# A hybrid attention and RWKV step on one core: half of the top-k rounds of three query tiles move behind attention's scores

## The chip, the cores and the metric

The kernel runs on one core of a Trainium2 chip. That core has five engines that work side by side, each through its own queue in order: TensorE (PE, matrix products and transposes), VectorE (DVE), ScalarE (ACT), GpSimd (POOL), and SyncE (SP), which here issues DMAs. The metric is the device time of one execution in microseconds (us); lower is better.

## The reference, cut to what matters

One layer of a streaming encoder is computed for 1024 prompt frames and 32 sample frames (1056 rows, in nine row tiles: tiles 0 to 7 of 128 prompt rows, tile 8 of the 32 sample rows).

```python
z = rms_norm(x) @ w_in                       # split into q, k, v, indexer q/k/w, RWKV inputs zs
# group A: sparse attention, 8 query heads, 4 key heads
score[t, s] = sum_h w[t, h] * relu(qi[t, h] . ki[s] / 8)     # admissible keys of the chunk only
keep the 256 best keys of each query (136 for the sample rows' 544 keys)
o_att = softmax(q . k / 8 over the kept keys) @ v
# group B: RWKV-7, 8 heads, a 64x64 state per head that goes through the frames in order
S = S * w_t - (S @ kk_t) b_t + v_t k_t ;  y_t = S @ r_t
h = x + concat(o_att, o_rwkv) @ w_out
y = h + square(relu(rms_norm(h) @ w_ff1)) @ w_ff2
```

For 1024 prompt keys the count kept is min(256, 1024/4) = 256; for the sample rows it is min(256, 544/4) = 136.

## The kernel before, in words

**Stages.** (1) Norm, transposes and the projection, all as products of a high and a low part (three matmuls for one); in it the indexer scores of tiles 2 to 8 (`idx_tile`), the q and k rows (`main2`, `norm_tile`) and the 14 blocks of RWKV inputs (`main3`, `zs_block`, L441 with the two evictions L450 and L451 on ACT). (2) Attention and RWKV side by side. (3) The output projection (L1310), then the feed-forward part (L1374, L1394), which is about half of the time and is not touched.

**Top-k by rounds.** The 256th best score of every row is found bit by bit. A round compares all scores of a tile with a candidate, counts, and sets one bit; there are 31 rounds after a first count. Two groups of tiles do it: `SLS[0]` = tiles 2, 3, 4 and 8 count on VectorE (L343, four counts a round), `SLS[1]` = tiles 5, 6 and 7 count on ScalarE as sums of signs (L363, three activations a round, over 768, 896 and 1024 columns). After the counts three small VectorE operations make the next candidate (L365, L366, L368). `step(1)` is called once behind each row tile of `main2` and each block of `main3` and advances both groups by one round. At the end of each group its masks are made: for tiles 5 to 7 a count, a compare and a minimum (L343, L382, L383), then signs and squares on ScalarE (L397, L398) and a prefix sum and a compare on VectorE (L403, L404), and last the mask `mb` itself (L405). `masks()` runs what is left of both groups before the joint loop of stage 2. In it the scores lie in the tile `G` (tiles 4 to 8), and the mask code works in `S.eq`, which lies in the pool from which RWKV's odd units take their tile `KB`; RWKV's odd units take their big tile `G` from the room of the scores.

**Attention** (`attn_all`) goes through 36 items, a head group j (0 to 3) and a row tile each: for each j the tiles in the order `ORD` = 8, 0, 1, 2, 3, 4, 5, 7, 6. At tile 8 and tile 0 of each j, `prep` loads and transposes that group's keys (L1116, L1118, L1121, L1122). An item makes scores (PE L1153, L1154; DVE L1156 with the mask; exp on ACT L1159), turns them (PE L1177; eviction L1178 on ACT or DVE) and multiplies by the values (L1193).

**RWKV** goes through five units (four of 256 frames, one of 32). Each has a front (gates, decays, the tiles `KB`, `AR`, the products L715 evicted by L718), a triangular inverse (`lane_inverse`: transposes L833 on DVE, 30 small steps L840 and L842 on POOL, transposes L845 and L846 on DVE), a finish on PE of tiny matmuls (L856, L862; DVE L857, L866, L871), a join (L771, L779), and a back with a serial chain over four chunks of 64 frames. `rwkv_tokens` turns the keys of a chunk for the back: eight transposes of 64 partitions (L749) in two groups, each with a copy of its own (L750).

**Order.** The code hands out one piece of attention and one piece of RWKV in turn (the loop at the end of `body`); a scheduler in the framework then fixes the order of each engine's queue by priorities and its own timing. Each queue is worked through in that order.

Of the kernel before, what the change touches and what calls it, by code (L numbers as in the profile page):

```python
# [151 lines left out]
def phase_a(S, pwx, pwy, pa, pi, px, xp, ps, late):  # L152
# [77 lines left out]
    S.sc, c = {}, 0  # L230
    for t in range(4, NT):
        n = 664 if t == 8 else 128 * (t + 1)
        S.sc[t] = G[:, c:c + n]
        c += n
# [3 lines left out]
    for SL in SLS:  # L238
        X = K()
        TK.append(X)  # L240
        X.SL, X.exact = SL, SL is SLS[0]
        for a, d in (("cnt", F32), ("nac", I32), ("cnd", I32), ("cns", F32), ("need", F32)):
            setattr(X, a, S.tk.tile([128, len(SL)], d, name=a + str(len(SL))))
        X.off = S.tk.tile([128, 2, len(SL)], F32, name="off" + str(len(SL)))
# [94 lines left out]
    def count(X, op, get, sc):  # L339
        for j, t in enumerate(X.SL):  # L340
            r = rows_of(t)
            n = S.sc[t].shape[1]
            nc.vector.tensor_scalar(junk[:r, :n], sc[t][:r, :n], get(j, r), None, op0=op, op1=ALU.add,  # L343
                                    accum_out=X.cnt[:r, j:j + 1])

    def topk(X):
# [9 lines left out]
        for i in range(30, -1, -1):  # L356
            if X.exact:
                count(X, ALU.is_lt, c_of, S.sc)
            else:
                for j, t in enumerate(X.SL):  # L360
                    r = rows_of(t)
                    n = S.sc[t].shape[1]
                    nc.scalar.activation(junk2[:r, :n], S.sc[t][:r, :n], AF.Sign, bias=c_of(j, r), scale=-1.0,  # L363
                                         accum_out=cnt[:r, j:j + 1])
            nc.vector.tensor_tensor(nac, cnt, X.off[:, 0] if X.exact else X.off[:, 1], op=ALU.is_gt)  # L365
# [26 lines left out]
        for j, t in enumerate(X.SL):  # L392
# [3 lines left out]
            cum = S.eq[j % 2][:r, :g.shape[1]]  # L396
# [61 lines left out]
    def main():  # L458
# [5 lines left out]
        for X in TK:  # L464
            nc.gpsimd.memset(X.cnt, 0.0)
            nc.gpsimd.memset(X.cns, 0.0)
            for j, t in enumerate(X.SL):
                n = S.sc[t].shape[1]
                for i in range(2):
                    nc.gpsimd.memset(X.off[:, i, j:j + 1], float(n - 256 - 256 * i))  # L470
# [83 lines left out]
    def masks():  # L554
        for g in tk:
            for _ in g:
                pass
# [317 lines left out]
def rwkv_back(S, rp, ps, U, state):  # L875
# [23 lines left out]
    for c in range(NC):  # L899
# [23 lines left out]
        for hp in range(4):  # L923
            for par in range(2):
                nc.tensor.matmul(pS[PAR[par], hp], KBs[:, par, hp], VU[:, par, hp], start=True, stop=True)  # L925
# [172 lines left out]
def attn_all(S, ap, ps):  # L1098
# [3 lines left out]
    items = [(j, t) for j in range(4) for t in ORD]  # L1102
# [40 lines left out]
    def scores(k, h):  # L1143
# [6 lines left out]
        for i, c0 in enumerate(range(0, n, 512)):  # L1150
# [5 lines left out]
            nc.vector.tensor_tensor_reduce(out=s[:, c0:c1], in0=pd, in1=S.mb[t][:, c0:c1], op0=ALU.add, op1=ALU.min, scale=-1.0,  # L1156
                                           scalar=m[:, 0:1] if i else FMAX, accum_out=m[:, i:i + 1])
        i = 1 if n > 512 else 0
        nc.scalar.activation(s, s, AF.Exp, bias=m[:, i:i + 1], scale=-1.0, accum_out=w.m[:, 6 + h:7 + h])  # L1159
# [44 lines left out]
    def begin(k):  # L1204
        j, t = items[k]
        if t == 8 or t == 0:
# [236 lines left out]
ORD = [8,0,1,2,3,4,5,7,6]  # L1443
# [21 lines left out]
def body(tc, I, O, dbg=None):  # L1465
# [4 lines left out]
    with pool(name="const") as cp, pool(name="dram", space=DRAM) as dp:  # L1470
# [16 lines left out]
        S.xs = mp.tile([128, 8, 64], F32R, name="mb7")  # L1487
        p1a, S.tk = opened("p1a", "right")
# [54 lines left out]
        for i in range(EARLYF, max(AHEAD, MA)):  # L1543
            if i == MA:
                masks()
            next(gr)
        if MA >= AHEAD:
            masks()
# [43 lines left out]
```

## Time and profile before

| | |
|---|---|
| median of 3 runs | 1783.88 us (1782.97 to 1784.06) |
| profiled execution | 1782.01 us |
| its span, first to last instruction | 1780.2 us |
| mean granted TensorE clock | 0.937 of full speed |
| busy: PE, DVE, ACT, POOL | 1667.3 us (94%), 913.7 us (51%), 711.4 us (40%), 533.1 us (30%) |

The times of runs agree within 0.1%. The profiled execution lies 1.8 us above its span and 1.9 us below the median. TensorE's clock has two levels, 1.2 and 2.4 GHz; a granted clock of 0.50 in a stretch means 1.2 GHz all through, 1.00 means 2.4 GHz. A matmul at 1.2 GHz is counted busy for longer, so that busy time times granted clock is the work at full speed.

### The profile page before, as it was taken

The page shows a single profiled execution, that of the slowest core. Times are in us where ns is not written, and L with a number is a line of the kernel's source. Part 1 is how long each engine was busy: PE and PEld are TensorE (multiplying, and loading weights), DVE is VectorE, ACT ScalarE, POOL GpSimd, SP SyncE. Part 2 cuts the span into 40 slices and gives each one's busy share as a digit, 9 for nine tenths or more (in the row PEclk, how much of TensorE's full clock was granted, in tenths as well). Part 3 has the DMA queues.
Part 4 walks back from the last instruction along what each step waited for, and adds up shares of the span by engine and source line. Part 5 has one row for each costly group of instructions (what it writes and reads, how often), then busy time and mean ns, then how long its engine had stood idle before and what let it go on. Part 6 is the DMA issues. An engine that isn't in the chain of part 4 may idle for free.

```text
span 1780.2 us, 32465 instructions
## 1 busy us (share of the span) xinstructions
PE 1667.3 (94%) x12966; PEld 1514.6 (85%) x12966; DVE 913.7 (51%) x2016; ACT 711.4 (40%) x1559; POOL 533.1 (30%) x759
## 2 busy tenths in 40 slices
PE   7999979987679999989989999999999999999999
PEld 6787769986557877767767799999999999999998
DVE  6476899975878586675643533232322222222224
ACT  6365567797555453434621331212222221212120
POOL 7568863453303031122210031212122222222110
PEclk9999989996669597988989999999999999999999
DMA  7211131323101102021234241111111111111105
GB/s 219 56 36 44 40 91 61 102 70 100 31 25 30 30 21 70 17 96 45 70 85 144 90 128 53 41 54 42 49 47 48 37 54 42 54 42 48 37 17 171
DMA packets 161087, 112.77 MB, mean 63 GB/s; under 512 B 31632, under 2 KB 150120, under 8 KB 160936
## 3 DMA queue, kind: packets, MB, share of 16 engines
q1 hardware_dynamic: 152104, 106.37, 20.5%
q10 hardware_dynamic: 8832, 4.33, 0.9%
q8 instruction: 102, 1.67, 0.4%
q14 instruction: 49, 0.40, 0.1%
HBM read 85.65 MB, written 25.01 MB: 62 GB/s over the span
## 4 chain that ended last, share of the span: by engine, by line
PE 50%; DMA 2%; ACT 1%; DVE 1%; issue 1%; SPq 0%; POOL 0%; ACTq 0%; DVEq 0%; POOLq 0%
PE pd L1374 20%; PE pr L1394 10%; PE pc L1394 5%; PE po L1394 5%; PE pd L1310 3%; PE pr L1310 2%; DMA of<-od 1%; PE po L1193 1%; DMA w1r<-in_w_ff_dram 0%; PE ptr L1177 0%; PE ptr L1408 0%; PE pc L925 0%; PE pd L1153 0%; PE ptr L145 0%; ACT G L1276 0%
## 5 line engine op out<-in xcount | busy, mean ns | idle before, releaser
L1374 PE MATMUL pd<-hh,w1h 128*128 128x352 f32 x768 | 248.0, 323 | 2.6 <-issue 1.5
L1374 PE MATMUL pd<-hh,w1l 128*128 128x352 f32 x768 | 247.6, 322 | 0.6 <-DVE w1l L1241 0.6
L1374 PE MATMUL pd<-hl,w1h 128*128 128x352 f32 x768 | 246.8, 321 | 0.0
L1380 DVE TENSOR_TENSOR h2l<-rl,h2h 128x352 fp32r<-128x352 f32 x96 | 56.8, 592 | 276.7 <-ACT h2h L1379 276.7
L1240 ACT CAST w2h<-w2r 128x512 fp32r<-128x512 f32 x64 | 39.8, 621 | 293.9 <-PE po L1394 144.7
L1378 POOL TENSOR_TENSOR rl<-rl 128x352 f32<-128x352 f32 x96 | 85.3, 889 | 214.8 <-ACT rl L1377 214.8
L1374 PEld LDWEIGHTS pd<-hh,w1h 128*128 128x128 f32 x768 | 144.1, 188 | 3.5 <-issue 1.8
L1374 PEld LDWEIGHTS pd<-hh,w1l 128*128 128x128 f32 x768 | 144.2, 188 | 0.9 <-DVE w1l L1241 0.9
L1374 PEld LDWEIGHTS pd<-hl,w1h 128*128 128x128 f32 x768 | 144.7, 188 | 0.0
L1241 POOL TENSOR_TENSOR w2l<-w2r,w2h 128x512 fp32r<-128x512 f32 x32 | 41.5, 1298 | 299.3 <-ACT w2h L1240 299.3
L1394 PE MATMUL pr<-h2h,w2l 128*128 128x352 f32 x384 | 124.3, 324 | 0.0
L1394 PE MATMUL pr<-h2h,w2h 128*128 128x352 f32 x384 | 124.3, 324 | 0.0
L1394 PE MATMUL pr<-h2l,w2h 128*128 128x352 f32 x384 | 124.1, 323 | 0.0
L363 ACT ACTIVATE AR<-G,cnd 128x768 bf16<-128x768 f32 (+2 forms) x93 | 96.8, 1040 | 42.4 <-DVE cnd L368 33.9
L1377 ACT ACTIVATE rl<-pd 128x352 f32<-128x352 f32 x96 | 44.3, 463 | 141.9 <-PE pd L1374 135.3
L1400 DVE TENSOR_TENSOR ya<-ya,pr 128x352 f32<-128x352 f32 x84 | 43.8, 521 | 100.6 <-PE pr L1394 100.6
L1177 PE MATMUL ptr<-ident,s 128*128 128x128 f32 (+2 forms) x328 | 66.3, 304 | 18.7 <-ACT s L1159 9.5
L1159 ACT ACTIVATE s<-s,m 32x544 f32<-32x544 f32 (+8 forms) x72 | 55.5, 771 | 56.2 <-DVE m L1156 54.5
L1379 ACT CAST h2h<-rl 128x352 fp32r<-128x352 f32 x96 | 46.6, 485 | 75.5 <-POOL rl L1378 75.5
L1394 PEld LDWEIGHTS pr<-h2l,w2h 128*128 128x128 f32 x384 | 72.3, 188 | 0.1
L1394 PEld LDWEIGHTS pr<-h2h,w2h 128*128 128x128 f32 x384 | 72.2, 188 | 0.1
L1394 PEld LDWEIGHTS pr<-h2h,w2l 128*128 128x128 f32 x384 | 72.3, 188 | 0.1
(452 smaller groups left out, 4573.6 us busy)
## 6 DMA issues: line engine op xcount, KB each, us to landing
w1r<-in_w_ff_dram SPq DMA_DIRECT2D x32, 512.0 KB, 4.2
w2r<-in_w_ff_dram SPq DMA_DIRECT2D x64, 256.0 KB, 2.8
zsd<-zm SPq DMA_DIRECT2D x12, 528.0 KB, 2.8
wraw<-in_w_in_dram SPq DMA_DIRECT2D x24, 256.0 KB, 2.7
wraw<-in_w_in_dram SPq DMA_DIRECT2D x40, 128.0 KB, 2.3
x<-in_x_prompt_dram SPq DMA_DIRECT2D x8, 512.0 KB, 4.9
hres<-hd ACTq DMA_DIRECT2D x16, 256.0 KB, 3.1
out_dram<-hres SPq DMA_DIRECT2D x16, 256.0 KB, 2.3
```

What stands on the lines that cost most here:

```text
L363: nc.scalar.activation(junk2[:r, :n], S.sc[t][:r, :n], AF.Sign, bias=c_of(j, r), scale=-1.0, accum_out=cnt[:r, j:j + 1])
L1159: nc.scalar.activation(s, s, AF.Exp, bias=m[:, i:i + 1], scale=-1.0, accum_out=w.m[:, 6 + h:7 + h])
L1177: nc.tensor.transpose(p[:x, i, h, :r], w.s[h][:, c0 + i * 128:c0 + i * 128 + x], S.ident[:r, :r])
L1241: (nc.vector if i % 2 else nc.gpsimd).tensor_tensor(lo, raw, hi.bitcast(F32), op=ALU.subtract)
L1310: nc.tensor.matmul(acc[:r], a[:, k], b, start=(i == 0), stop=(i == 23))
L1374: nc.tensor.matmul(acc, a[:, k], m[:, k, o:o + n], start=(i == 0), stop=(i == 23))
L1377: nc.scalar.activation(rl, acc, AF.Relu)
L1378: nc.gpsimd.tensor_tensor(rl, rl, rl, op=ALU.mult)
L1379: nc.scalar.copy(h2h[:, o:o + n], rl)
L1380: nc.vector.tensor_tensor(h2l[:, o:o + n], rl, h2h[:, o:o + n].bitcast(F32), op=ALU.subtract)
L1394: nc.tensor.matmul(acc, a[:, k], m[:, o:o + n], start=(i == 0), stop=(i == 11))
L1400: nc.vector.tensor_tensor(y, y, acc, op=ALU.add)
```

## The change

Five edits go together.

1. The scores of tiles 5, 6 and 7 get a tile of their own, `late`, that lives as long as the masks; `G` holds only tiles 4 and 8. Room for it comes from a smaller DMA scratch area (`dynamic_dma_scratch_size=1024`).
2. The rounds of tiles 5 to 7 are advanced at every second call of `step` only, 16 steps (a first count and 15 rounds) in place of 32. The other 16 rounds and the masks become a generator `gm` in the joint loop: one piece at every fifth turn, queued on DVE and ACT behind the last scores and the last exp that were handed out (`issue_after`). Its scratch comes from attention's pool (`junk`, and the tiles `s`, which attention's scores also use).
3. Attention's items get another order, `PASSES`: j = 0 and 1 with tiles 8, 0 to 4 only, j = 2 and 3 with all tiles, then j = 0 and 1 with tiles 5, 7, 6. The keys of j = 0 and 1 are loaded and turned a second time for that (two more `prep`).
4. The exact rounds on VectorE keep the count of scores at or above the candidate and need two small operations in place of three.
5. `rwkv_tokens` turns the keys of both parities at once: four transposes of 128 partitions and one copy of 512 columns per chunk, in place of eight of 64 and two copies of 256.

```diff
     G = S.tk.tile([128, 4096], F32, name="G")
-    for t in range(4, NT):
-        n = 664 if t == 8 else 128 * (t + 1)
-        S.sc[t] = G[:, c:c + n]
+    S.sc, c = {4: G[:, 0:640], 8: G[:, 640:1304]}, 0
+    for t in SLS[1]:
+        n = 128 * (t + 1)
+        S.sc[t] = S.late[:, c:c + n]
...
         for i in range(30, -1, -1):
             if X.exact:
-                count(X, ALU.is_lt, c_of, S.sc)
+                count(X, ALU.is_ge, c_of, S.sc)
+                nc.vector.tensor_scalar(nac, cnt, 255.5, float(1 << i), op0=ALU.is_lt, op1=ALU.mult)
+                nc.vector.scalar_tensor_tensor(cnd, nac, (1 << i) >> 1, cnd, op0=ALU.bitwise_xor, op1=ALU.bitwise_xor)
+                yield
+                continue
...
-                    nc.scalar.activation(junk2[:r, :n], S.sc[t][:r, :n], AF.Sign, bias=c_of(j, r), scale=-1.0,
+                    j2 = junk2 if i > LATE else S.at.tile([128, 1024], BF16, name="junk", bufs=1)
+                    nc.scalar.activation(j2[:r, :n], S.sc[t][:r, :n], AF.Sign, bias=c_of(j, r), scale=-1.0,
...
-                e = S.eq[j % 2][:r, :n]
+                e = S.at.tile([128, 1024], F32, name="s", bufs=XPB)[:r, :n]
...
-    left = [32 - EARLY * (len(IDXO) - EI), 32]
+    left, calls = [32 - EARLY * (len(IDXO) - EI), 31 - LATE], [0]
     def step(n):
+        calls[0] += 1
         for i, g in enumerate(tk):
-            m = min(n, left[i])
+            m = min(n if i == 0 else calls[0] % 2, left[i])
...
     def masks():
-        for g in tk:
-            for _ in g:
-                pass
+        for _ in tk[0]:
+            pass
+        return tk[1]
...
-    KBs = rp.tile([128, 2, 4, 64], F32, name="KBs", bufs=TOKB)
+    KBs = rp.tile([128, 4, 2, 64], F32, name="KBs", bufs=TOKB)
-    for par in range(2):
-        p = ps.tile([128, 4, 64], F32, name=TOKP[0], bufs=TOKP[1])
-        for hp in range(4):
-            nc.tensor.transpose(p[:, hp], U.KB[PAR[par], c, hp].rearrange("p a b -> p (a b)"), S.ident[PAR[par], PAR[par]])
-        nc.scalar.copy(KBs[:, par], p)
+    p = ps.tile([128, 4, 2, 64], F32, name=TOKP[0], bufs=TOKP[1])
+    for hp in range(4):
+        nc.tensor.transpose(p[:, hp].rearrange("p a b -> p (a b)"), U.KB[:, c, hp].rearrange("p a b -> p (a b)"), S.ident)
+    nc.scalar.copy(KBs, p)
...
-    items = [(j, t) for j in range(4) for t in ORD]
+    items = [(j, t) for j, s in PASSES for t in s]
...
+        S.pace = v.ins, a.ins
...
+EARLIER, LATER = (8, 0, 1, 2, 3, 4), (5, 7, 6)
+PASSES = ((0, EARLIER), (1, EARLIER), (2, EARLIER + LATER), (3, EARLIER + LATER), (0, LATER), (1, LATER))
+LATE = 15
+PACE = 5
...
-        gens = [ga, gr]
+        gens, turns = [ga, gr, gm], 0
         while gens or wo is None:
+            turns += 1
             for g in list(gens):
+                if g is gm:
+                    if turns % PACE == 0 or ga not in gens:
+                        with tc.issue_after(S.pace[0]), tc.issue_after(S.pace[1]):
+                            if next(g, 1) == 1:
+                                gens.remove(g)
+                    continue
```

Three places show what the order of the queues becomes. The first is ACT's queue where the projection ends. `zm` and `tm` are the last evictions of RWKV inputs, `AR<-G` the sign counts of tiles 5 to 7, `tmp<-k` and `tmp<-pr` the first steps of RWKV's second unit. Before:

```order
L451 ACTIVATE tm<-acc,pv 96x351
L363 ACTIVATE AR,cnt_121<-G,cnd_123 128x768
L363 ACTIVATE AR,cnt_121<-G,cnd_123 128x896
L363 ACTIVATE AR,cnt_121<-G,cnd_123 128x1024
L363 ACTIVATE AR,cnt_121<-G,cnd_123 128x768
L636 ACTIVATE tmp<-k,pv 128x256 x4
L363 ACTIVATE AR,cnt_121<-G,cnd_123 128x896
L632 ACTIVATE tmp<-pr,hv 128x256 x2
```

Now, at the same place:

```order
L458 ACTIVATE tm<-acc,pv 96x351
L644 ACTIVATE tmp<-k,pv 128x256 x4
L640 ACTIVATE tmp<-pr,hv 128x256 x4
L640 ACTIVATE tha<-pr,hv 128x256 x4
L672 ACTIVATE Ep<-D_4707 128x1040
```

The sign counts are gone from there, and RWKV's second unit follows the evictions directly.

The second place is DVE's queue around the end of the finish of RWKV's first unit (`X` is its last transpose). `KB` with `need` or a scan is mask work of tiles 5 to 7 before; the operations on `KB<-k` and `KB<-tha` are the second unit's. Before:

```order
L871 STREAM_TRANSPOSE X_5393<-G 32x512
L400 TENSOR_SCALAR need_125<-need_125 128x1
L1200 TENSOR_TENSOR t_5691<-t_5691,po 128x128
L404 SCALAR_TENSOR_TENSOR KB<-KB,need_125,G 128x1024
L1163 RECIPROCAL m<-m 128x2
L1141 SCALAR_TENSOR_TENSOR Q<-ptr,Q 64x256
L1178 COPY ph<-ptr 128x256
L684 TENSOR_TENSOR KB<-k,D_4838 64x4x4x64
```

Now, between the same finish's first eviction (L864) and its last transpose (L878), `cnt`, `nac` and `cnd` belonging to one late round:

```order
L864 TENSOR_TENSOR L<-pr,lm 128x512
L1164 ISA s,m<-pd,mb_73 128x256
L1164 ISA m 128x1
L1164 ISA s,m<-pd,mb_73 128x256
L1164 ISA m 128x1
L1172 RECIPROCAL m<-m 128x2
L1209 TENSOR_TENSOR t_5451<-t_5451,po 128x128
L372 TENSOR_TENSOR nac_123<-cnt_122,off_127 128x3
L373 SCALAR_TENSOR_TENSOR cnd_124<-nac_123,cnd_124 128x3
L375 TENSOR_SCALAR cnd_124<-cnd_124 128x3
L873 TENSOR_TENSOR G<-pr,Yl 32x16x32 x4
L878 STREAM_TRANSPOSE X_5221<-G 32x512 x2
```

The wide mask operations have left this place; three small ones of a round have come. The second unit's `KB` now stands before the finish.

The third place is ACT's queue during the first pass of attention, where `junk<-late` are the sign counts of two late rounds and `s` the exps of tiles 3 and 4. Now:

```order
L1167 ACTIVATE s,m<-s,m 128x512 x2
L370 ACTIVATE junk,cnt_122<-late,cnd_124 128x768
L927 COPY VU<-pc 64x256
L370 ACTIVATE junk,cnt_122<-late,cnd_124 128x896
L1148 ACTIVATE Q<-ptr 64x256
L1208 COPY t_5674<-po 128x128
L1187 COPY ph<-ptr 128x512
L370 ACTIVATE junk,cnt_122<-late,cnd_124 128x1024
L1167 ACTIVATE s,m<-s,m 128x640
L370 ACTIVATE junk,cnt_122<-late,cnd_124 128x768
L370 ACTIVATE junk,cnt_122<-late,cnd_124 128x896
L370 ACTIVATE junk,cnt_122<-late,cnd_124 128x1024
```

Before, no count stood among the exps of these tiles; now three stand behind the exps of most items of the first two passes.

## Rows read from the trace of the kernel before

**Rows 1.** Windows by stage: us, busy and count of PE, PEld, DVE, ACT, POOL; clock; DMA.

```profile
209.00:414.00 205.00, 183.77 (x1081) 174.66 (x1079) 175.92 (x475) 163.21 (x353) 99.33 (x119) 0.95 0.26 79
414.00:483.00 69.00, 43.56 (x242) 36.47 (x241) 55.77 (x133) 40.03 (x90) 28.56 (x45) 0.56 0.25 67
483.00:525.00 42.00, 27.84 (x363) 20.85 (x362) 30.26 (x70) 21.30 (x49) 4.13 (x6) 0.58 0.09 26
525.00:573.00 48.00, 45.16 (x641) 34.54 (x643) 40.15 (x93) 29.13 (x64) 15.20 (x38) 1.00 0.06 17
573.00:678.00 105.00, 101.64 (x1260) 82.39 (x1259) 71.21 (x182) 51.95 (x126) 22.62 (x47) 0.80 0.15 42
678.00:774.00 96.00, 92.46 (x1263) 74.70 (x1255) 65.38 (x166) 44.66 (x119) 17.69 (x46) 0.86 0.17 50
774.00:850.00 76.00, 69.90 (x1074) 54.14 (x1073) 42.74 (x109) 28.97 (x81) 15.34 (x42) 0.84 0.19 56
850.00:905.00 55.00, 52.33 (x823) 40.11 (x821) 35.97 (x90) 33.31 (x75) 14.14 (x13) 1.00 0.20 63
```

**Rows 2.** PE's waits from 205 to 416 us: total, times, longest.

```profile
PE acc L441 <- ACT tm L451: 14.1, 7, 7.7
```

**Rows 3.** PE's waits from 414 to 530 us.

```profile
PE pr L793 <- ACT tmp L636: 10.3, 1, 10.3
PE ptr L1177 <- ACT s L1159: 8.6, 4, 5.4
```

**Rows 4.** Sign counts on ACT (ns min/median/max, first and last start); its one table load.

```profile
L363 ACT ACTIVATE AR<-G,cnd x93: 919/1042/1156, 208.2 to 451.9; 128x768 bf16<-128x768 f32 x31, 128x896 bf16<-128x896 f32 x31, 128x1024 bf16<-128x1024 f32 x31
...
L133 ACT ACT_TABLE_LOAD x1 | 1.3, 1283 | 0.7 <-PEq L1581 0.7
```

**Rows 5.** Timeline, 414 to 480 us, RWKV's first inverse (start, us).

```profile
414.87 3.23 DVE L684 TENSOR_TENSOR KB<-k,D 64x1024 f32<-64x1024 f32 x1 [0.42 <-ACT zm L450]
...
422.67 0.36 SPq L612 DMA_DIRECT2D k<-zsd  x1
...
426.96 0.93 ACT L363 ACTIVATE AR<-G,cnd 128x768 bf16<-128x768 f32 x1 [8.39 <-DVE cnd L368]
...
427.90 1.69 ACT L636 ACTIVATE tmp<-k,pv 128x256 f32<-128x256 f32 x4
...
434.92 0.79 PE L629 MATMUL pr<-wa,w 96*128 96x256 f32 x2 [1.29 <-ACT tmp L632]
...
457.16 0.22 POOL L840 TENSOR_TENSOR tl<-Yl 128x15 f32<-128x15 f32 x1 [14.44 <-DVE cnd L366]
...
477.04 0.32 POOL L842 TENSOR_TENSOR Yl<-Yl,tl 128x15 f32<-128x15 f32 x1
...
479.30 1.08 DVE L845 STREAM_TRANSPOSE Yl<-L 128x512 f32<-128x512 f32 x1
```

**Rows 6.** DVE's timeline, 458 to 503 us: mask work of tiles 5 to 7, finish.

```profile
458.71 1.01 DVE L343 TENSOR_SCALAR_CACHE_REDUCE AR<-G,cnd 128x768 bf16<-128x768 f32 x1
...
487.47 1.75 DVE L403 TENSOR_TENSOR_SCAN KB<-ones,KB 128x768 f32<-128x768 f32 x1
...
496.83 2.28 DVE L403 TENSOR_TENSOR_SCAN KB<-ones,KB 128x1024 f32<-128x1024 f32 x1
...
500.84 0.69 DVE L871 STREAM_TRANSPOSE X<-G 32x512 f32<-32x512 f32 x1
501.70 1.26 DVE L404 SCALAR_TENSOR_TENSOR KB<-KB,need,G 128x1024 f32<-128x1024 f32 x1
```

**Rows 7.** Lines of finish and join on PE: ns min/median/max, first and last start.

```profile
L856 PE MATMUL pr<-L,G x640: 191/191/258, 483.1 to 853.1; 32*32 32x32 f32 x160
...
L771 PE MATMUL pr<-X,G x256: 191/191/258, 525.2 to 805.1; 32*32 32x32 f32 x128
```

**Rows 8.** PE's timeline: four transposes of 128 and of 64 partitions.

```profile
457.19 0.66 PE L1118 MATMUL ptr<-ident,k 128*128 128x128 f32 x4
...
458.97 0.46 PE L749 MATMUL pr<-ident,KB 64*128 64x64 f32 x4
```

More of the change, by code (lines that the diff above doesn't have):

```diff
@@ L243, in phase_a @@
             setattr(X, a, S.tk.tile([128, len(SL)], d, name=a + str(len(SL))))
-        X.off = S.tk.tile([128, 2, len(SL)], F32, name="off" + str(len(SL)))
+        X.off = S.tk.tile([128, len(SL)], F32, name="off" + str(len(SL)))
     ones = S.tk.tile([128, 1], F32, name="ones")
@@ L342, in count @@
             n = S.sc[t].shape[1]
-            nc.vector.tensor_scalar(junk[:r, :n], sc[t][:r, :n], get(j, r), None, op0=op, op1=ALU.add,
+            jk = junk if X.exact or not hasattr(S, "at") else S.at.tile([128, 1024], BF16, name="junk", bufs=1)
+            nc.vector.tensor_scalar(jk[:r, :n], sc[t][:r, :n], get(j, r), None, op0=op, op1=ALU.add,
                                     accum_out=X.cnt[:r, j:j + 1])
@@ L395, in topk @@
             a = [x[:r, j:j + 1] for x in (cnt, cns, need)]
-            cum = S.eq[j % 2][:r, :g.shape[1]]
+            cum = (S.eq[j % 2] if X.exact else S.at.tile([128, 1024], F32, name="s", bufs=XPB))[:r, :g.shape[1]]
             nc.scalar.activation(g, g, AF.Sign, bias=a[1], accum_out=a[0])
@@ L464, in main @@
         for X in TK:
-            nc.gpsimd.memset(X.cnt, 0.0)
+            nc.gpsimd.memset(X.cnt, 255.75 if X.exact else 0.0)
             nc.gpsimd.memset(X.cns, 0.0)
@@ L468, in main @@
                 n = S.sc[t].shape[1]
-                for i in range(2):
-                    nc.gpsimd.memset(X.off[:, i, j:j + 1], float(n - 256 - 256 * i))
+                nc.gpsimd.memset(X.off[:, j:j + 1], float(n - 512))
         Wa = wprep("x", [(1536, 72), (768, 256)], 328, False)
@@ L924, in rwkv_back @@
             for par in range(2):
-                nc.tensor.matmul(pS[PAR[par], hp], KBs[:, par, hp], VU[:, par, hp], start=True, stop=True)
+                nc.tensor.matmul(pS[PAR[par], hp], KBs[:, hp, par], VU[:, par, hp], start=True, stop=True)
         sn = rp.tile([128, 4, 64], F32, name="st", bufs=3)
@@ L1101, in attn_all @@
     nc, I, O = S.nc, S.I, S.O
-    items = [(j, t) for j in range(4) for t in ORD]
+    items = [(j, t) for j, s in PASSES for t in s]
+    turned = {(j, s[0] if s[0] != 8 else 0) for j, s in PASSES}
     J, W = {}, {}
@@ L1154, in scores @@
             nc.tensor.matmul(pd, X[:, h, :r], B[:, c0:c1], start=False, stop=True)
-            nc.vector.tensor_tensor_reduce(out=s[:, c0:c1], in0=pd, in1=S.mb[t][:, c0:c1], op0=ALU.add, op1=ALU.min, scale=-1.0,
-                                           scalar=m[:, 0:1] if i else FMAX, accum_out=m[:, i:i + 1])
+            v = nc.vector.tensor_tensor_reduce(out=s[:, c0:c1], in0=pd, in1=S.mb[t][:, c0:c1], op0=ALU.add, op1=ALU.min, scale=-1.0,
+                                               scalar=m[:, 0:1] if i else FMAX, accum_out=m[:, i:i + 1])
         i = 1 if n > 512 else 0
-        nc.scalar.activation(s, s, AF.Exp, bias=m[:, i:i + 1], scale=-1.0, accum_out=w.m[:, 6 + h:7 + h])
+        a = nc.scalar.activation(s, s, AF.Exp, bias=m[:, i:i + 1], scale=-1.0, accum_out=w.m[:, 6 + h:7 + h])
+        S.pace = v.ins, a.ins
     def inverse_sums(k):
@@ L1205, in begin @@
         j, t = items[k]
-        if t == 8 or t == 0:
+        if t == 8 or (j, t) in turned:
             prep(j, t == 8)
@@ L1487, in body @@
         S.xs = mp.tile([128, 8, 64], F32R, name="mb7")
+        S.late = mp.tile([128, sum(128 * (t + 1) for t in SLS[1])], F32, name="late")
         p1a, S.tk = opened("p1a", "right")
@@ L1543, in body @@
         for i in range(EARLYF, max(AHEAD, MA)):
-            if i == MA:
-                masks()
             next(gr)
-        if MA >= AHEAD:
-            masks()
+        gm = masks()
         S.G.append(S.tk.tile([128, 2, 4, 4, 128], F32, name="G"))
         raw = wo = None
-        gens = [ga, gr]
+        gens, turns = [ga, gr, gm], 0
         while gens or wo is None:
+            turns += 1
             for g in list(gens):
+                if g is gm:
[4 more added lines that the diff above has]
+                    continue
                 with (tc.high_priority(OFF) if g is gr else nullcontext()):
```

6 lines of the change are left out of this document (2 added, 4 removed).

## The prediction

> **What bounds the kernel now.** I read the windows by stage first, then PE's waits in the stages that lose time, then the timeline of the stage that loses most. Busy time times granted clock gives PE's work at full speed. From 525 to 905 us the five rows of [rows 1] give 45.2 + 81.3 + 79.5 + 58.7 + 52.3 = 317.0 us of such work in 380 us, a rate of 0.834; PE is busy nearly all through, and what is lost is mostly the lower clock (0.80 to 0.86 in three of the five). From 414 to 525 us it is 24.4 + 16.1 = 40.5 us of work in 111 us: PE waits, and runs at a clock of 0.56 to 0.58 while it works. From 209 to 414 us it is 174.6 in 205 us. So the place with room is the change of stages between 414 and 525 us, and it lies where the sign counts and masks of tiles 5 to 7 end.
>
> Why it is slow there stands in the timeline [rows 5]. RWKV's first unit gets its tile KB at 414.87, when the projection's last eviction is out. ACT then stands 8.39 us before a sign count, because the candidate comes late from DVE, and the second unit's first step (L636) stands behind it in ACT's queue until 427.90; PE waits 10.3 us for it [rows 3]. Three more counts lie between the steps that follow, and PE's last product of that group starts at 434.92. Only behind it come the products that fill the first unit's G. GpSimd's inverse therefore starts at 457.16, having stood 14.44 us, and runs to 477.36; its result waits in DVE's queue until 479.30. The finish starts at 483.1 and the join at 525.2 [rows 7]. In between DVE does mask work: 15 wide operations, the first at 458.71 and the last at 501.70, 20.3 us together [rows 6]; two scans and two compares, the first of them at 487.47, lie between the finish's evictions (5.9 us), a scan of 2.28 us before its last transposes, which end at 501.53.
>
> **The change, part by part.**
>
> *Fewer counts beside the projection.* PE's waits for ACT's evictions from 205 to 416 us come to 14.1 us [rows 2]. One round of signs is three counts at 1.04 us, 3.1 us of ACT; the 31 rounds start between 208.2 and 451.9 us, so that by their share of that time some 26 lie before 414 [rows 4]. Of the 31, 15 stay ahead of attention. ACT is 163 of 205 us busy [rows 1]; with 11 rounds fewer in this stretch (34 us) it is 129. I take 7 us, half of the 14.1: 11 of the 26 rounds go, and those that stay come at every second call only. Bounds: nothing, and all 14.1. The third small operation that exact rounds lose on DVE is counted at nothing by itself, since PE does the projection beside it; if it does show, it is inside the same bound.
>
> *No counts and masks between projection and join.* Step by step. k is issued at 422.67; if it lands by 425.5 (an estimate: no later than 427.90 it must have), so L636 gains 2.4 us of its 427.90; the counts between the next steps go (3.1 us), so G is complete 5.5 us earlier, and its transposes find DVE a little emptier (1 us): the inverse starts near 451 and ends near 471. The 1.9 us in DVE's queue behind it go too: finish near 474 in place of 483.1. From finish to the end of the last transposes before took 18.4 us, of which 8.2 were masks and about 0.6 their small companions; now 9.6, so near 484. The join came 23.7 us after that, because at half clock PE had 106 matmuls of attention beside the inverse's own 256 in between; by the new order 52 stand there, and the join comes near 490: 35 us earlier. Not all of that is won: those matmuls come later. Half of the 16.1 us of work between finish and join moves behind it, 7.7 us, which at 0.834 costs 9.2. Net 26 us. Bounds: 10 us, if the order's other neighbours keep the join back, since the finish alone is 9 earlier; and 45 us, if PE also gets its full clock sooner (it is busy 71.4 us from 414 to 525 at about 0.57, so half clock alone costs 31 there).
>
> *The late rounds and masks beside attention.* 16 rounds bring 50 us of counts to ACT, and the masks 20.3 us of wide DVE work, into a stretch that has PE busy 147 of 153 us, ACT 81 and DVE 111 (525 to 678, [rows 1]). By the order the rounds fill the first two passes of attention; ACT goes there from half busy to near nine tenths, and an exp that PE needs can stand behind up to three counts. The trace of before shows counts beside PE-bound work: 209 to 414 us, where 26 rounds go with 14.1 us of PE's waits [rows 2], 0.54 us a round. That makes 9 us for 16 rounds, 10 with a little for attention's shorter items. DVE's mask work then comes beside RWKV's fronts: DVE has 42 of 153 us free, so I add nothing for the 20 us, and price it in the range. Value 10 us lost; bounds 0, and 50 if every count stands in PE's way. The waits that the new DVE operations bring (a candidate behind three counts on ACT) stand in front of score operations, which PE's next transposes need; they are inside the same bound.
>
> *Key transposes.* Five units have 17 chunks (four of four and one of one). A chunk has two groups of four transposes of 64 partitions at 0.46 us, and now one group of 128 partitions at 0.66 us [rows 8]: 34 x 0.46 - 17 x 0.66 = 4.4 us less for PE. The second turning of the keys for j = 0 and 1 adds 16 of the latter, 2.6 us. Net 1.8 us of PE work, 2 us at the rate above. ACT's copies become fewer, where it is not the bound. The loads for the second turning are hidden by the item before, as those of j = 1 to 3 were; if not, a few us at the end, in the range.
>
> *Sum.* Against the profiled execution, 1782.0 us: - 7 - 26 + 10 - 2 = - 25, that is 1757.0. Its span is 1780.2, so the span would be near 1755. The median of the runs lies 1.9 us above the profiled execution: **1759 us**. What is late next is PE itself, at the rate of the middle stage. Behind 905 us nothing changes except which engine's last piece ends the stage.
>
> **The rivals.**
>
> *Larger gain by the clock* (0.13). If attention's early items and RWKV's second front keep PE busy while the inverse runs, the 31 us of half clock go to a third and the counts hide: 1759 - 20 - 5 = 1734. For it: in [rows 1] the clock is 1.00 as soon as PE is dense (525 to 573). Against: the first passes have the small tiles, and PE waited there 8.6 us for exps [rows 3], which is not the masks' doing alone.
>
> *The start is not freed* (0.09). KB still waits for the projection's end, and the inverse still takes 20.2 us of GpSimd. If the join comes only the 10 us earlier of the lower bound, the sum is - 7 - 10 + 10 - 2 + 9 (the skipped work) = 0: 1784. For it: the wait for exps in [rows 3] is attention's own.
>
> *ACT becomes the bound of the first passes* (0.14), slower. 50 us of counts beside exps and evictions, in one queue in order: if they stand in PE's way one after the other, and PE so falls back to the lower clock, the 10 us become 50: 1799. It decides from 35 us on, since that eats up the 25 us. For it: ACT at nine tenths, and a count in ACT's queue held everything behind it for 8.39 us once [rows 5]. Against: the pieces are spread over every fifth turn, behind an exp and not ahead of it.
>
> *Table loads* (0.03), slower. Sign now stands between Exp, Tanh and copies. A switch on each side of 16 rounds at 1283 ns would be 41 us: 1800. Against: the trace has one load in the whole execution [rows 4], with Sign beside Tanh already [rows 5]. The Trainium skill (ScalarE: Activation LUTs, "Table sets: the hidden batching unit") has the rule that speaks against such mixing: group activations by table set. It puts a switch at about 2.66 us, so an estimate by that page would be 85 us; the trace shows no switch, and the rule does not bite unless the sets differ.
>
> **How the numbers follow.** The forecast has 0.61, for 1740 to 1777. 0.2% of the median, 3.6 us, is about what a measurement can tell from no change. Faster takes the forecast, the larger gain and a third of the unfreed start: 0.77. Slower takes ACT as the bound and the table loads, less a little of the former that ends even: 0.15. Within 0.2%: 0.08. The range goes from 1727, below the larger gain, to 1793, short of the slower cases' full price: it leaves out about 0.17.
>
> **What would show it.** Right: no L636-like wait of 10 us; the first finish (L863) near 468 (474 less the 7) and the first join (L778) near 483; ACT's counts scattered over 460 to 640 us with ACT at 0.8 or more, and PE's waits for exps there under 20 us. The steady rate near 0.83. Wrong: a join still beyond 505; PE's waits for `s` or `ph` behind ACT of 30 us or more before the third pass; clock rows at 0.5 over most of the first two passes; more than one table load.

## The result, and the profile after

The changed kernel takes 1792.66 us (median of 20 runs, 1784.46 to 1799.58) beside 1783.01 us of the kernel before (20 runs). The ratio is 1.0052, 95% interval 1.0039 to 1.0064: slower by 0.5%, some 9.3 us, where 24 us faster were forecast. The time lies just inside the upper edge of the range (1793). The execution that was profiled, 1784.46 us, is the fastest of the 20, so its trace shows 2.5 us of the loss and not 9.3. What is read from it below are steps and rates; what an edit costs comes from ratios of many runs.

These are the stages of the changed kernel (columns as in [rows 1]). The three middle cuts of [rows 1] are the finishes of the second to fourth unit; here they are the joins behind them; the other cuts are the same events. In order: end of the projection of RWKV's inputs, first finish, first join, second join, third join, fourth join, fifth finish, last attention item, start of the feed-forward part.

```profile
209.00:404.00 195.00, 182.01 (x1081) 174.82 (x1079) 160.72 (x414) 129.57 (x287) 102.04 (x119) 0.96 0.27 83
404.00:469.00 65.00, 40.70 (x226) 34.09 (x225) 48.97 (x95) 28.96 (x68) 30.91 (x46) 0.62 0.28 78
469.00:488.00 19.00, 13.81 (x321) 11.55 (x323) 12.65 (x46) 11.31 (x27) 3.67 (x3) 0.59 0.07 21
488.00:581.00 93.00, 81.32 (x1040) 65.06 (x1034) 61.28 (x165) 65.16 (x154) 20.13 (x45) 0.71 0.10 26
581.00:682.00 101.00, 88.62 (x1199) 70.78 (x1196) 77.14 (x194) 58.34 (x142) 20.98 (x47) 0.83 0.16 43
682.00:775.00 93.00, 88.77 (x1182) 68.28 (x1175) 65.33 (x158) 44.36 (x109) 16.39 (x46) 0.89 0.20 62
775.00:824.00 49.00, 47.84 (x627) 37.04 (x627) 32.22 (x85) 25.23 (x58) 12.63 (x36) 0.97 0.13 37
824.00:930.00 106.00, 101.26 (x1146) 77.89 (x1144) 59.24 (x153) 49.52 (x105) 19.10 (x21) 0.98 0.22 62
930.00:1025.00 95.00, 84.74 (x389) 66.84 (x389) 40.36 (x61) 24.18 (x46) 6.73 (x9) 0.95 0.38 121
```

The head start is there. The projection ends 10 us earlier (404 in place of 414), the first finish comes at 469.0 and the first join at 487.6, which the lines of finish and join show (ns min/median/max, first and last start):

```profile
L863 PE MATMUL pr<-L,G x640: 191/236/258, 469.0 to 828.4; 32*32 32x32 f32 x160
...
L778 PE MATMUL pr<-X,G x256: 191/191/254, 487.6 to 776.1; 32*32 32x32 f32 x128
```

In [rows 7] they stood at 483.1 and 525.2. So RWKV is 38 us ahead at its first join. At its last finish (beginning of the 824 row; 849.6 before) it is 25 us ahead, and attention, which ended at 902 before, ends at 930, 28 us late. Busy time times clock shows the middle's rate, work per time: from 488 to 581 us 81.32 x 0.71 = 57.7 us of work in 93, a rate of 0.62; the rows from 581 to 824 give 199.0 in 243, 0.82; the row to 930 gives 99.2 in 106, 0.94. From the first join to the last attention item that is 355.9 in 442, 0.805, where the 0.834 of [rows 1] was taken to hold.

Three more places of the changed kernel. First, PE's waits beside the projection (209 to 404 us), where [rows 2] had 14.1 us:

```profile
PE acc L448 <- ACT tm L458: 10.5, 5, 3.8
```

Second, the sign counts on ACT (ns, first and last start): 45 beside the projection, 48 beside attention.

```profile
L370 ACT ACTIVATE junk<-late,cnd x48: 919/1042/1161, 446.0 to 626.6; 128x768 bf16<-128x768 f32 x16, 128x896 bf16<-128x896 f32 x16, 128x1024 bf16<-128x1024 f32 x16
...
L370 ACT ACTIVATE AR<-late,cnd x45: 927/1043/1167, 208.2 to 312.3; 128x768 bf16<-128x768 f32 x15, 128x896 bf16<-128x896 f32 x15, 128x1024 bf16<-128x1024 f32 x15
```

Third, PE's waits from 930 to 1025 us, where the output projection waits for the last attention tile to be split:

```profile
PE pd L1319 <- ACT o L1305: 8.9, 1, 8.9
```

The same wait was 4.8 us before. From 1025 us on nothing differs (757.4 us to the end, 758.0 before).

### The profile page after: what moved, and what is told of

Same layout as the page of the kernel before. It is cut to its first block, busy times and chain, and to the rows that moved or that the text cites. A ratio compares the mean times of both kernels' runs of the same rounds, so it can differ in the third digit from the quotient of the medians.

```text
span 1782.7 us, 32330 instructions
## 1 busy us (share of the span) xinstructions
PE 1669.6 (94%) x12914; PEld 1516.2 (85%) x12914; DVE 908.7 (51%) x1990; ACT 709.1 (40%) x1546; POOL 539.6 (30%) x756
## 4 chain that ended last, share of the span: by engine, by line
PE 63%; DVE 6%; ACT 4%; issue 1%; DMA 1%; POOL 1%; SPq 0%; DVEq 0%; ACTq 0%; POOLq 0%
PE pd L1383 20%; PE pr L1403 10%; PE pc L1403 5%; PE po L1403 5%; PE pd L1319 3%; PE po L1202 2%; PE pr L1319 2%; PE ptr L1186 2%; PE pr L723 1%; PE pd L1161 1%; ACT junk L370 1%; PE pd L1162 1%; PE pc L917 1%; DVE L L840 1%; PE pc L913 1%
## 5 line engine op out<-in xcount | busy, mean ns | idle before, releaser
L1174 POOL COPY x<-m 128x128 f32<-128x128 f32 (+1 forms) x36 | 11.2, 310 | 203.8 <-DVE m L1172 189.3
```

## The experiments

Two theories stood against each other at first. *Crowding*: the late rounds and masks cost PE more than the 10 us taken. *Order*: the new item order costs it, small tiles in a row first and large tiles without RWKV at the end. Ratios are to the kernel before, on the same chip, with their 95% interval; 0.001 is 1.8 us.

**Edits 4 and 5 alone (e_keys_two).**

```diff
 # the kernel before, with
...
+nc.vector.scalar_tensor_tensor(cnd, nac, (1 << i) >> 1, cnd, op0=ALU.bitwise_xor, op1=ALU.bitwise_xor)
...
+KBs = rp.tile([128, 4, 2, 64], F32, name="KBs", bufs=TOKB)
...
```

> The kernel before with edits 4 and 5 alone (two-operation exact rounds, key transposes for both parities). Both main theories (crowding: the late rounds and masks cost PE more than the 10 us taken; order: the new item order costs it) expect the same here: 4.4 us of PE work less at a rate near 0.85, 1778 to 1782 beside 1783 of before, never slower. The rival that the small edits themselves bring the loss expects 1786 or more.

Measured 1781.42 us, 0.9978 (0.9963 to 0.9993). The small edits gain about 3.9 us; they aren't the cause.

**All rounds and masks early, order new (e_order).**

```diff
-            m = min(n if i == 0 else calls[0] % 2, left[i])
+            m = min(n, left[i])
...
-LATE = 15
+LATE = -1
...
-        gm = masks()
+        for _ in masks():
+            pass
```

> The changed kernel with all rounds and masks ahead of attention as in the kernel before; item order, second key turning and edits 4 and 5 stay. Crowding theory: the start is as before (first finish near 480, first join near 522), the middle loses nothing, 1780 to 1785. Order theory: the small tiles in a row and the large tiles without RWKV beside them cost on their own; 1790 to 1802, with the stretch from the first join to the last attention item at a lower rate than before's 0.83.

Measured 1814.01 us, 1.0168 (1.0154 to 1.0182), beyond both. The run doesn't price the order, since it brings a wait of its own. The mask work still has its scratch in attention's three `s` tiles, and now stands ahead of the first item. On DVE's timeline (start, us), attention's first score operation comes behind it, at 493.67; in the changed kernel it is at 440.1.

```profile
485.61 1.75 DVE L410 TENSOR_TENSOR_SCAN s<-ones,s 128x768 f32<-128x768 f32 x1
...
492.56 1.12 DVE L411 SCALAR_TENSOR_TENSOR s<-s,need,late 128x896 f32<-128x896 f32 x1
493.67 0.67 DVE L1164 CUSTOM_DVE_ANT_0 s<-pd,mb 32x512 f32<-32x512 f32 x1
```

**Late rounds left out (e_norounds).**

```diff
-        for i in range(30, -1, -1):
+        for i in range(30, -1 if X.exact else LATE, -1):
```

> The changed kernel with the 16 late rounds of tiles 5 to 7 left out (48 sign counts and the DVE steps between them aren't computed; the masks of these tiles are made from the bits found till then). Crowding theory: 50 us of ACT work go out of the middle, 10 to 20 us faster than the changed kernel, 1772 to 1782. Order theory: within 4 us of the changed kernel, 1788 to 1793.

Measured 1783.78 us, 1.0001 (0.9986 to 1.0015): 0.0051 or 9.1 us less than the changed kernel. So 16 rounds cost 9 us beside attention, which is what the forecast took (10). That is just short of what crowding expected and more than order did; the rounds are a part of the loss, not all.

**Late rounds and masks, order of before (e_late_old).**

```diff
-PASSES = ((0, EARLIER), (1, EARLIER), (2, EARLIER + LATER), (3, EARLIER + LATER), (0, LATER), (1, LATER))
+PASSES = tuple((j, EARLIER + LATER) for j in range(4))
...
-if turns % PACE == 0 or ga not in gens:
+if turns > 2 or ga not in gens:
```

> The changed kernel with the item order of the kernel before (each j with all nine tiles, keys turned once), and the late rounds and masks handed out one piece in every turn so that they end ahead of the first large tile. Order theory: the freed start is kept and the loss of the order goes, 1770 to 1780. Crowding theory: the same 50 us of counts and 20 us of masks stand closer together, so PE waits more at the first pass: 1785 to 1800.

Measured 1823.47 us, 1.0223 (1.0201 to 1.0245), worse than crowding expected. The window from the first to the second join:

```profile
493.00:577.00 84.00, 57.17 (x865) 48.56 (x865) 55.16 (x136) 59.14 (x117) 17.01 (x35) 0.60 0.05 13
```

PE is busy 57 of 84 us at a clock of 0.60. On ACT's timeline (start, us) attention starts no exp for 83 us between these two, while the rounds run on to 550.8 and the masks' first part behind them; attention's next score operation comes on DVE at 575.24.

```profile
494.95 0.63 ACT L1168 ACTIVATE s<-s,m 128x384 f32<-128x384 f32 x1
...
578.49 0.71 ACT L1168 ACTIVATE s<-s,m 128x512 f32<-128x512 f32 x1
```

So the run says what a stopped attention costs, and not what the old order costs with late masks.

**The new order on the kernel before (e_passes).** As e_keys_two, and the order with its second key turning; masks have their scratch outside attention's pool.

```diff
...
-    items = [(j, t) for j in range(4) for t in ORD]
+    items = [(j, t) for j, s in PASSES for t in s]
...
```

> The kernel before with edits 4 and 5 and the new item order (with the second key turning), rounds and masks where they were, with their scratch outside attention's pool as in the kernel before. The run with the order alone moved the masks' scratch into attention's pool, where the first item waited 43 us for it; here that wait is away. Order theory: 1790 to 1800, 10 to 20 us over the 1781 of edits 4 and 5. Crowding theory (masks and rounds beside RWKV make the loss): only the second turning's 2.6 us show, 1782 to 1786.

Measured 1795.11 us, 1.0061 (1.0039 to 1.0083): 0.0083 or 14.8 us over edits 4 and 5. The order, with its second turning of keys, makes a kernel as slow as the changed one, with no late work in it. The two have their first join within 2 us of each other (523.2 and 525.1), so the windows from the first join to the second can be laid side by side. Edits 4 and 5:

```profile
523.00:607.00 84.00, 74.70 (x1118) 59.64 (x1117) 63.82 (x156) 43.81 (x105) 20.01 (x45) 0.90 0.12 31
```

With the new order:

```profile
525.00:612.00 87.00, 73.39 (x1031) 59.89 (x1030) 57.87 (x138) 38.64 (x97) 20.41 (x46) 0.76 0.12 30
```

RWKV's unit takes nearly as long (84 and 87 us), but PE gets 55.8 us of work done in place of 67.2: 87 matmuls fewer. In the old order the large tiles of j = 0 stand beside RWKV for the first half of this window (their exps start from 527 to 563 us), and small tiles of j = 1 behind them; in the new one it is small tiles nearly all through. The 11.4 us of work come later.

The clock falls too, from 0.90 to 0.76, but that can't be put down to the order. With the old order the same work was done in this window at 0.75 by edit 5 alone (the run e_keys below, 67.3 us of work) and at 0.81 by the kernel before (66.6):

```profile
522.00:620.00 98.00, 89.77 (x1124) 72.03 (x1124) 64.88 (x158) 45.08 (x109) 20.50 (x46) 0.75 0.10 27
```

```profile
525.00:612.00 87.00, 82.19 (x1130) 66.04 (x1130) 63.25 (x157) 44.63 (x108) 20.05 (x45) 0.81 0.12 30
```

What the order costs shows in the whole stretch from the projection's end to the feed-forward part. Edits 4 and 5:

```profile
414.00:1016.00 602.00, 533.52 (x6084) 421.93 (x6085) 387.40 (x919) 273.57 (x631) 125.95 (x247) 0.85 0.21 61
607.00:712.00 105.00, 99.78 (x1280) 80.72 (x1278) 71.42 (x174) 49.35 (x121) 21.11 (x47) 0.83 0.15 42
```

With the new order:

```profile
416.00:1035.00 619.00, 537.56 (x6097) 427.81 (x6097) 394.29 (x923) 274.61 (x635) 127.10 (x251) 0.85 0.21 61
612.00:705.00 93.00, 83.98 (x1188) 68.06 (x1184) 66.60 (x157) 43.15 (x110) 19.45 (x44) 0.87 0.16 44
```

These two executions took 1776.14 and 1794.09 us. Of the 17 us more in this stretch, PE stands idle for 13 (81.4 in place of 68.5 us) and is busy for 4; the clock is 0.85 in both. Nor is the mean clock of the whole execution lower over all runs: the median is 0.9385 with the new order (6 runs) and 0.938 without (12). The idle time grows in several places: from 9.3 to 13.6 us in the window between the first two joins, from 5.2 to 9.0 us in the one behind it, and from 5.3 to 7.7 us in front of the output projection. No single wait stands out.

**No late work at all (e_nolate).** Late rounds and masks left out.

```diff
+                for u in SLS[1]:
+                    nc.gpsimd.memset(S.mb[u], 0.0)
...
-        return tk[1]
+        return iter(())
```

> The changed kernel with the 16 late rounds and also all mask work of tiles 5 to 7 left out (their masks are zeros written beside the projection). Leaving out the rounds alone gave 9 us. Crowding theory: the masks' DVE work and their use of attention's s tiles cost another 10 to 20 us, 1762 to 1774. Order theory: 0 to 5 us more, 1778 to 1784, since small tiles in a row leave PE waiting anyway.

Measured 1773.11 us, 0.9931 (0.9910 to 0.9953): 0.0070 or 12.5 us under the run without rounds. That is crowding's figure: the masks cost something, though the forecast gave them nothing (the two intervals leave some 5 us either way). Beside e_passes, which has the same order, it is 0.0130 or 23.2 us: that is what the freed start is worth at the end, when nothing is put in its place. Its first join is at 488.7, 36.4 us ahead of e_passes.

**Postponed items between j = 2 and j = 3 (e_mid).**

```diff
-PASSES = ((0, EARLIER), (1, EARLIER), (2, EARLIER + LATER), (3, EARLIER + LATER), (0, LATER), (1, LATER))
+PASSES = ((0, EARLIER), (1, EARLIER), (2, EARLIER + LATER), (0, LATER), (1, LATER), (3, EARLIER + LATER))
```

> The changed kernel with the postponed large tiles of j = 0 and 1 between j = 2 and j = 3 in place of the end; same work. Tail theory (what is postponed costs because RWKV has ended by then): the last attention item comes earlier beside RWKV, 1783 to 1788, 5 us or more under the changed kernel. If PE does the postponed items at its full rate at the end anyway (clock 0.98, busy 0.95 there), 1790 to 1795.

Measured 1785.86 us, 1.0003 (0.9978 to 1.0028), 0.0049 under the changed kernel: the end's part seems worth some 9 us. It isn't the wait in front of the output projection, which is as long here as in the changed kernel:

```profile
PE pd L1319 <- ACT o L1305: 8.7, 1, 8.7
```

**Only j = 0 split, pieces at every third turn (e_split1).**

```diff
-PASSES = ((0, EARLIER), (1, EARLIER), (2, EARLIER + LATER), (3, EARLIER + LATER), (0, LATER), (1, LATER))
+PASSES = ((0, EARLIER), (1, EARLIER + LATER), (2, EARLIER + LATER), (3, EARLIER + LATER), (0, LATER))
...
-PACE = 5
+PACE = 3
```

> The changed kernel with only j = 0 split (its large tiles last, j = 1 to 3 with all nine tiles, one second turning of keys instead of two) and the late pieces at every third turn in place of every fifth, so that they end ahead of the first large tile. Order theory: half of the order's loss comes back, 1782 to 1788. Crowding theory: the pieces stand closer, 1793 to 1805.

Measured 1806.62 us, 1.0115 (1.0085 to 1.0144): as crowding said, or a little more. It changes two things at once, though, and the order's part in it isn't told apart.

**Edit 5 alone (e_keys).** The key transposes of e_keys_two without the two-operation rounds.

> The kernel before with edit 5 alone (key transposes for both parities). Edits 4 and 5 together gave -3.9 us (ratio 0.9978). If PE's 4.4 us less work are the cause, this has all of it: ratio 0.997 to 0.9985. If it is the third DVE operation that the exact rounds lose, 0.9995 to 1.001.

Measured 1775.13 us, 0.9955 (0.9931 to 0.9979): the gain is the key transposes'. The interval overlaps that of edits 4 and 5, so edit 4 is told apart neither from nothing nor from a small loss.

**Large and small tiles in turn (e_mix).** Edits 4 and 5, and

```diff
...
-ORD = [8,0,1,2,3,4,5,7,6]
+PASSES = ((0, (8, 0, 1, 2, 3, 4, 5, 7, 6)),) + tuple((j, (8, 7, 0, 6, 1, 5, 2, 4, 3)) for j in (1, 2, 3))
```

> The kernel before with edits 4 and 5, and for j = 1 to 3 large and small tiles in turn (8, 7, 0, 6, 1, 5, 2, 4, 3); j = 0 as before, nothing turned twice. Order theory in the form that small tiles in a row leave PE waiting: 5 to 12 us better than the 1781 of edits 4 and 5, ratio 0.991 to 0.995. Order theory in the other form, that only the amount of attention work left when RWKV ends counts: this is nearly unchanged, ratio 0.997 to 0.999.

Measured 1776.84 us, 0.9951 (0.9928 to 0.9975). Between the two forms, and it has to be seen beside edit 5's 0.9955: mixing later passes brings nothing that shows.

**Only the masks late, order of before (e_masks_late).** The order of e_late_old, and

```diff
...
-LATE = 15
+LATE = -1
...
-if turns % PACE == 0 or ga not in gens:
+if turns % 4 == 0 and turns > 2 or ga not in gens:
```

> The changed kernel with all rounds ahead of attention, the item order of the kernel before, and only the masks of tiles 5 to 7 late (one piece at every fourth turn, ahead of the first large tile). If the masks in the start are what holds it and the order is what costs, the join comes near 500 without the order's price: ratio 0.990 to 0.996. If mask work costs 12 us wherever it stands beside RWKV, 0.998 to 1.003. If the first large tile waits for its mask, 1.005 or more.

Measured 1785.04 us, 0.9998 (0.9974 to 1.0022). The first join comes at 503.0, 20 us ahead of e_keys_two, and the time isn't better than that one's 0.9978: masks moved beside RWKV cost about what they free.

**The order's cost once more (e_pass_mid, e_pass_one).** e_passes with the order of e_mid, and with that of e_split1.

> As the run of edits 4 and 5 with the new item order on the kernel before (ratio 1.0061), but with the postponed large tiles of j = 0 and 1 between j = 2 and j = 3 in place of the end. If the order's cost is what is left for the time after RWKV has ended, it mostly stays, since as much attention is left then: 1.003 to 1.007. If it is the last stretch's waits between attention and projection (tiles 5 to 7 ready last), most of it goes: 0.998 to 1.002, as the same move gave the changed kernel 9 us.

Measured 1786.80 us, 1.0015 (1.0001 to 1.0030), 0.0046 under e_passes, as much as the same move gave in e_mid. e_passes waits 7.7 us in its last stretch (PE's waits, 895 to 1034 us):

```profile
PE pd L1314 <- ACT o L1300: 7.7, 1, 7.7
```

In e_pass_mid that wait is gone; PE is busy 83 of 86 us there:

```profile
944.00:1030.00 86.00, 83.45 (x391) 65.68 (x390) 40.22 (x61) 24.19 (x46) 6.76 (x9) 1.00 0.44 134
```

Its window from first to second join stays slow (55.1 us of work in 90):

```profile
525.00:615.00 90.00, 75.49 (x1002) 61.45 (x996) 58.47 (x138) 39.20 (x99) 20.81 (x47) 0.73 0.11 29
```

> The same kernel with only the large tiles of j = 0 postponed, to the end; one second key turning. If each postponed item costs, half of the order's 15 us: ratio 1.001 to 1.003. If only the position of the very last items counts, all of it: 1.005 to 1.007. If it is the two passes of small tiles in a row, nothing: 0.997 to 0.999.

Measured 1803.64 us, 1.0090 (1.0069 to 1.0111). It refutes that each postponed item costs its share: half as many cost no less. Its expectation had an error of its own: with j = 0 alone split, the small tiles of j = 0 and j = 1 still follow each other, so that it does not take away the small tiles in a row. Why it is above e_passes is open; its trace doesn't show more waiting. From the projection's end to the feed-forward part PE is idle for 71.2 us, less than in e_passes, but busy for 555.8 us at a lower clock:

```profile
416.00:1043.00 627.00, 555.76 (x6087) 438.00 (x6088) 390.11 (x920) 273.90 (x633) 127.05 (x249) 0.83 0.20 60
```

**Edit 5 with mixed tiles (e_keys_mix).**

> The kernel before with edit 5 alone and large and small tiles in turn for j = 1 to 3; the candidate against both kernels. Edit 5 alone gave 0.9955, edits 4 and 5 with this order 0.9951, edits 4 and 5 without it 0.9978. If the order adds to edit 5: 0.991 to 0.994; if not, 0.9945 to 0.997.

Measured 1776.81 us, 0.9957 (0.9938 to 0.9975): the mix adds nothing to edit 5.

**A fourth s tile (e_s4, e_keys_s4, e_mid_s4).**

```diff
-XPB = 3
+XPB = 4
```

> The changed kernel with four s tiles in place of three. Leaving out the mask work as well as the late rounds gave 12.5 us more than the rounds alone. If the masks cost because they hold s tiles that attention's scores need: 5 to 12 us better than the changed kernel, ratio 0.998 to 1.002. If it is DVE's and ACT's time in their queues: within 3 us of it, 1.003 to 1.007.

Measured 1790.30 us, 1.0031 (1.0005 to 1.0056), in the second theory's interval of 1.003 to 1.007, and its interval overlaps that of the changed kernel: if the masks cost by holding `s` tiles, it is little.

> Control for the fourth s tile: the kernel before with edit 5 alone and four s tiles (room from the smaller DMA scratch area). Edit 5 alone gave 0.9955. If s tiles are short only where masks use them, as before: 0.994 to 0.997. If attention is short of them anyway, 0.988 to 0.993.

Measured 1782.69 us, 0.9983 (0.9961 to 1.0005), above both: attention isn't short of such tiles. The run also has the smaller DMA scratch area of edit 1. Beside edit 5's 0.9955 it is 0.0028 slower, which the two intervals do not tell from nothing; what that area costs in the changed kernel is untested.

> The changed kernel with four s tiles and the postponed large tiles between j = 2 and j = 3 (alone 1.0003). If both causes are separate and as sized, 0.994 to 0.997, faster than before; if the fourth tile brings nothing, 0.999 to 1.002.

Measured 1791.29 us, 1.0030 (1.0008 to 1.0051), missed by both. Beside e_s4 the move of the postponed items gives nothing here. So the 9 us of e_mid are seen in two pairs of three, and what the end is worth stays uncertain.

## Why the prediction was wrong

The runs make a ladder from the kernel before to the changed one, each rung a difference of two ratios (each good to some 3 to 6 us), beside the forecast's term. The measured rungs add up by the way they are made; the third also takes in edit 1's tile and its smaller scratch area.

| rung | forecast | measured |
|---|---|---|
| edits 4 and 5 (e_keys_two) | -4.4 us | -3.9 us |
| item order, second key turning (e_passes) | +2.6 | +14.8 |
| freed start, nothing late (e_nolate) | -7 - 26 = -33 | -23.2 |
| masks late (e_norounds) | 0 | +12.5 |
| rounds late (the changed kernel) | +10 | +9.1 |
| sum | -25 | +9.3 |

**What failed first: the item order was priced at its second turning of keys, 2.6 us.** It costs 14.8. The sum took the middle's rate of 0.834 [rows 1] as a property of the stage and charged only work postponed at the start at it. But that rate was made with large tiles beside RWKV's second unit. With small tiles there PE does 55.8 us of work in place of 67.2, and it stands idle for 13 us more before the feed-forward part. RWKV's chain gains little from the emptier PE: the last product of its finishes starts at 836.8 in place of 844.9 us, while the last attention item ends 57 us later (951.5 and 894.5). This was shown with no late work in the kernel; the same stretch of the changed kernel has 57.7 us of work. Which of the waits makes the 13 us isn't told apart, and e_pass_one shows that an order can also cost by a lower clock.

**What failed second: "DVE has 42 of 153 us free, so I add nothing for the 20 us".** The masks cost 12.5 us. By which way is open. The traces without masks (e_nolate) and with them (e_norounds), from the projection's end to the feed-forward part:

```profile
409.00:1012.00 603.00, 533.27 (x6098) 422.51 (x6099) 374.84 (x873) 251.60 (x590) 132.01 (x251) 0.86 0.22 63
```

```profile
406.00:1025.00 619.00, 544.68 (x6099) 431.57 (x6100) 390.84 (x909) 260.58 (x606) 133.41 (x251) 0.84 0.21 61
```

For practically the same matmuls (6098 and 6099) PE is idle 4.6 us longer (74.3 and 69.7) and busy 11.4 us longer, at a lower clock; over all runs of the two the median clock is 0.939 and 0.9435. So added waiting, in DVE's queue or elsewhere, is the smaller part in these traces, and why the clock is lower isn't shown. That the shared `s` tiles are not the cause is what e_s4 speaks for.

**The freed start was found near where it was forecast, in part by luck, and was worth less.** First finish 469.0 (forecast 468), first join 487.6 (483); GpSimd's inverse starts at 445.13 (451, or 444 with the 7 us of the projection). But the prediction had the second unit's first step behind the sign counts, and its first sign of being right, no wait like that of 10 us, did not come. No count is left there, and PE still waits 9.7 us (10.3 before):

```profile
PE pr L800 <- ACT tmp L644: 9.7, 1, 9.7
```

```profile
412.68 0.36 SPq L620 DMA_DIRECT2D k<-zsd  x1
...
416.38 1.71 ACT L644 ACTIVATE tmp<-k,pv 128x256 f32<-128x256 f32 x4 [11.15 <-DVE AR L692]
```

The step needs the load of `k`, issued at 412.68 us, which takes 3.6 us to land; DVE's operations on `AR`, which the profile names, end at the same moment. From the projection's last eviction to this step it is 11.2 us in place of 12.7, so the counts held it by 1.5 us and not by 2.4. From that eviction to the inverse's start the change gains 2 us, where 6.5 were forecast; the projection's end gains 10 in place of 7, and so the places fit. (In the other traces with the same projection it ends between 406 and 409 us, so part of the 10 may be chance.) The larger part, from finish to join, was right: 18.6 us in place of 42.1. It hangs on the masks and not on the item order: with masks late and the old order (e_masks_late) it is 19.1 us, with masks early and the new order (e_passes) 42.9.

Of the 36.4 us between the joins of e_passes and e_nolate 23.2 reach the end. The forecast let 33 arrive of 42; it took off 9.2 us for postponed work, and the runs lose 13.2 on the way. (Half of 16.1 is 8.05 and not 7.7, which would make the 9.2 to 9.7.)

**"Behind 905 us nothing changes except which engine's last piece ends the stage"** left out the wait of 8.9 us in front of the output projection, 4 us longer than before. e_passes without it in e_pass_mid is 8 us better, but e_mid is 9 us better with it, so that wait isn't shown to be what the end costs.

**What was right.** The price of the rounds, from [rows 2] (0.54 us a round), held: 9.1 for 10, good to some 3.5 us. By which waits isn't shown, and ACT did not fill up as forecast: from 460 to 640 us it is busy 124.80 of 180, 0.69 where 0.8 or more was expected. The rival that ACT becomes the bound had the sign and nearly the time (1799), but not the cause. No switch of tables came: the changed kernel too has one load in its whole execution.

```profile
L133 ACT ACT_TABLE_LOAD x1 | 1.3, 1283 | 0.7 <-PEq L1599 0.7
```

That signs stand between exps and tanhs without a switch is the trace's reading. The Trainium skill (ScalarE: Activation LUTs, "Table sets: the hidden batching unit") has exp and tanh share a set, and this trace agrees.

**A kernel that beats both.** Edit 5 alone, 0.9955 (0.9931 to 0.9979), 8 us below the kernel before and 17 below the changed one; the runs with mixed tiles (0.9951, 0.9957) can't be told from it.

## What to carry to other kernels

A rate read in a stage belongs to the pairs of work that ran there: whoever changes which items stand beside a serial chain must price the rate anew. Here the chain gained 8 us from the emptier PE, and the stage lost 17. An engine's mean free time is no cover for moved work: 20 us of masks beside an engine with 42 us free cost 12.5. Before several edits go in together, run those that have nothing to do with the idea alone: here one small edit did better alone than with the rest. And compare a lower clock in one window with other kernels that do the same work there, and with the whole stretch, before calling it the cause.

## What the runs showed of the hardware

The same work can stand at quite different clocks. With the old order PE did 67.2, 67.3 and 66.6 us of work at full speed between the first two joins, in busy times of 74.70, 89.77 and 82.19 us at granted clocks of 0.90, 0.75 and 0.81 (e_keys_two, e_keys, the kernel before). So busy time times clock tells the work and busy time alone does not, and one window's clock is no mark of its item order: e_keys, with 0.75, is among the fastest kernels here.

A kernel's times go with the mean granted clock of the execution: e_masks_late ran from 1770.39 us at 0.946 to 1791.96 us at 0.931, and the kernel before, in 17 runs beside e_passes, from 1776.36 us at 0.943 to 1797.74 us at 0.929. The profiled execution of e_masks_late was the fastest of its twelve; single executions of these variants say nothing about a few microseconds.
